# Modulation weights as the moving operand, and the mixer's shift added to z, in a one-core hybrid encoder layer

## The chip, the cores and the metric

The kernel runs on one core of a Trainium2 chip. The time is device microseconds (us) of one execution of the whole program. The times before are 2665.93, 2655.82 and 2659.03 us, median 2659.03.

## What is computed

One encoder layer over two request groups, 2048 and 512 positions of 1024 channels (2560 columns in all), with one modulation vector per group:

```python
mod = (silu(c) @ w_ada + b_ada)
shift1, scale1, gate1, shift2, scale2, gate2 = split(mod, 6)
h = rmsnorm(x, g_mix_norm) * (1 + scale1) + shift1
z = h @ w_in
y_f = fourier_mixer(z[..., :512], w_fourier, b_fourier)
y_s = s5_mixer(z[..., 512:], a, log_dt, b, c, d, w_glu, b_glu)
merged = concat([rmsnorm(y_f), rmsnorm(y_s)])
x = x + gate1 * (merged @ w_out)
h = rmsnorm(x, g_mlp_norm) * (1 + scale2) + shift2
ff = square(relu(h @ w_mlp_in + b_mlp_in)) @ w_mlp_out + b_mlp_out
x = x + gate2 * ff
y = rmsnorm(x, g_final)
```

`w_ada` is 1024 x 6144, `w_in` and `w_out` are 1024 x 1024, the MLP's matrices 1024 x 4096 and back. Results are float32; most products are formed from a high and a low half of each operand (three TensorE matmuls each, lines 229 to 231, from a CAST on ScalarE, L225, and a difference on VectorE, L226).

## The kernel before

Channels lie on partitions, positions along the free axis. The instructions of all stages are written in Python and then ordered, engine by engine, by a list scheduler with a time model of its own, so that an edit in one place can move instructions in another. The stages, with where they lie in the profiled execution:

- **The mixer's start** (`mix_in`, 0 to about 342 us). `ada1` computes the first 16 columns of 128 of the modulation (shift1 in `mod[:, 0:8]`, scale1 in `mod[:, 8:16]`) in four groups `j` of 512 outputs: the two columns of `cs` (silu of c) are the stationary operand, the weights move (L705), the [2, 512] result is copied out (L707) and turned by four transposes (`pat`, L710), VectorE adds the bias (L711). After the fourth group come `gs1` (L712) and `sh4`. `ssm_params` and `ssm_pre` make the tables of the S5 mixer (`Ir`, `Ii`, `O`, `cbi`, `Dm` and others; lines 159 to 319). `zs(it, t)` makes z for one of five tiles of 512 positions, order 4, 0, 1, 2, 3: per k of 8 a scale by `gs1` and the row factor `rb` (L829), then h = x + shift as high half on ScalarE (L831) and low half on VectorE (L832), then 4 x 8 x 3 matmuls into `ps`, a copy to `z` and a store. `folds` prepares the Fourier half with `wfold`'s folded weights `wf`. Loads of the first tile and of `w_in` wait on GpSimd `gate` copies that read a column of `mod` of group `j`, so that they start behind the modulation's weights; `JD = 2` is the group for those that name none.
- **The S5 stage** (about 342 to 660 us). `run` goes over blocks `q` of the S5 mixer (`lead`, `step1` to `step3`: psV, psY) and calls `slot` between them, which runs one `ada_slot` and one unit of `beside` (`fourier`: px, pyc, pys, pc; then `out_f`: pof, which lasts to 762 us). `ada(j)`, j = 16 to 47, makes one more column of 128 of the modulation: eight products of 128 x 128 weights (stationary) with the two columns of `cs` (L687; each product shows as two matmuls in the trace), bias by VectorE (L688). Its weights `wa` are 512 KB a load, `AB = 2` buffers, and `ada_slot` loads the weights of j + 2 after it has used those of j.
- **The mixer's end** (`mix_out`, about 762 to 1020 us): GELU, GLU (`pgate`), the output projection (`pf`/`pout` at L1220 and L1224). `precombine` (L1258 loads, L1263 GpSimd sums, L1264 stores) makes 32 pieces of the MLP's combined weights here, in tiles `q`, while others still wait.
- **The MLP** (`mlp`, from about 1020 us): seven-product (Strassen) blocks; per step a weight load `wr` (L1394), its halves `wh` (ScalarE, L1404) and `wl` (VectorE, L1406), matmuls `pf` and `acc`. In the first block the low halves are also stored (`wL`, L1408). `x` is first scaled and shifted (L1324, L1325), then split into `th` (L1356, L1357). The remaining 12 pieces of `precombine` run in the first block, in slices of a tile `big` (`pre2`); where their loads stand in the queue of SP is left to the scheduler.

Of the kernel before, what the change touches and what calls it, by code (L numbers as in the profile page):

```python
# [26 lines left out]
AB = 2  # L27
# [3 lines left out]
XB = 2  # L31
WB = 4
U0 = 6
JD = 2
XK = 2
CB = 2
NB = 4
# [522 lines left out]
class Net:  # L560
# [3 lines left out]
    def run(self):  # L564
        tc, nc, A = self.tc, self.nc, self.A
        with ExitStack() as es:
# [23 lines left out]
            spps, spp = pool("spp", "right")  # L590
            fes, fe = pool("fe", "right")
            self.Ze = [fe.tile([96, n], F32R, name="Ze%d" % n) for n in (352, 256)]
            self.aj, self.wa = 16, {}
            self.pcs = [(w, c) for w in range(2) for c in range(16)]
            P = self.mix_in(spp)
            sas, sa = pool("ssa", "right")
# [6 lines left out]
            for q in range(nb + 2):  # L603
                if q < nb:
                    bl.append(S.lead(q))
                    self.slot(gen)
                if 1 <= q <= nb:
                    S.step2(bl[q - 1])
                if q >= 2:
                    self.slot(gen)  # L610
                    S.step3(bl[q - 2])
                    self.slot(gen)
                if q < nb:
                    S.step1(bl[q])
                    self.slot(gen)
            self.pull(gen, 1000)
            self.banks(7)
            sps.close()
# [61 lines left out]

    def ada(self, j):
        nc = self.nc
        v3 = lambda n: self.v[n].unsqueeze(2).broadcast_to([128, 8, 2])
        ps = self.ps([128, 2], "pa")
        w = self.wa.pop(j)
        for k in range(8):
            nc.tensor.matmul(ps, w[:, k], self.cs[:, k], start=k == 0, stop=k == 7)  # L687
        nc.vector.tensor_scalar(self.mod[:, j], ps, self.v["b_ada"][:, j:j + 1], None, op0=ALU.add)  # L688
        if j == 39:
            nc.vector.scalar_tensor_tensor(self.gs2, self.mod[:, 32:40], 1.0, v3("g_mlp_norm"), op0=ALU.add, op1=ALU.mult)  # L690
        if j == 47:
            nc.vector.tensor_scalar(self.ng2, self.mod[:, 40:48], -1.0, None, op0=ALU.mult)
            nc.vector.tensor_tensor(self.gb2, self.mod[:, 40:48], v3("b_mlp_out"), op=ALU.mult)

    def ada1(self, tp):

        nc = self.nc
        v3 = lambda n: self.v[n].unsqueeze(2).broadcast_to([128, 8, 2])
        for j in range(4):
            ps = self.ps([2, 512], "pa")  # L700
            for k in range(4):
                w = tp.tile([128, 2, 512], F32, tag="wa", name="wa", bufs=WB)
                nc.sync.dma_start(w, self.A["w_ada1"][j, k])
                for i in range(2):
                    nc.tensor.matmul(ps, self.cs[:, 2 * k + i], w[:, i], start=k + i == 0, stop=k + i == 4)  # L705
            r = tp.tile([2, 512], F32, tag="ar", name="ar")
            nc.scalar.copy(r, ps)  # L707
            pt = self.ps([128, 4, 2], "pat")
            for i in range(4):
                nc.tensor.transpose(pt[:, i], r[:, 128 * i:128 * i + 128], self.ident[:2, :2])  # L710
            nc.vector.tensor_tensor(self.mod[:, 4 * j:4 * j + 4], pt, self.v["b_ada"][:, 4 * j:4 * j + 4].unsqueeze(2).broadcast_to([128, 4, 2]), op=ALU.add)  # L711
        nc.vector.scalar_tensor_tensor(self.gs1, self.mod[:, 8:16], 1.0, v3("g_mix_norm"), op0=ALU.add, op1=ALU.mult)  # L712
        nc.vector.tensor_scalar(self.sh4, self.mod[:, 0:8], 4.0, None, op0=ALU.mult)

    def ada_slot(self):
        j = self.aj
        if j < self.aend:
            self.ada(j)
            if j + AB < self.aend:
                self.ada_load(self.adp, j + AB, AB)  # L720
            self.aj += 1

    def ada_open(self, tp, end):
# [34 lines left out]
    def mix_in(self, spp):  # L758
# [5 lines left out]
        with ExitStack() as es:  # L764
# [9 lines left out]
            def load(t):  # L774
                xs[t] = xp.tile([128, 8, 4, 130], F32, tag="xq", name="xq")
                if t != order[0]:
                    self.gate(xs[t][:1, 0, 0, 0:1], t == order[1])
                    nc.sync.dma_start(xs[t][:, :, :, 0:128], A["xq"][t].rearrange("p k (s n) -> p k s n", s=4))
                    return
                for k in range(0, 8, XK):  # L780
                    self.gate(xs[t][:1, k, 0, 0:1], j=0)
                    nc.gpsimd.dma_start(xs[t][:, k:k + XK, :, 0:128], A["xq"][t][:, k:k + XK].rearrange("p k (s n) -> p k s n", s=4))

            def norm(t):
# [20 lines left out]
            pre = pres.enter_context(tc.tile_pool(name="pre", bufs=1, side="right"))  # L805
            with tc.tile_pool(name="mir", bufs=1) as rp:
                with tc.tile_pool(name="tp0", bufs=1, side="right") as tp0:
                    self.ada1(rp)
                    P = ssm_params(nc, tc, spp, po, pre, tp0, A)
                    load(4)  # L810
                    norm(4)
                    ws = [wp.tile([128, 8, 512], F32R, name="wi%d" % i) for i in range(2)]
                    for k in range(0, 8, 2):
                        raw = rp.tile([128, 2, 512], F32, name="raw", bufs=2)
                        self.gate(raw[:1, 0, 0:1], k < 4, 0)
                        nc.gpsimd.dma_start(raw, A["w_in"][1, :, k:k + 2])
                        split(nc, ws[0][:, k:k + 2], ws[1][:, k:k + 2], raw)
            def zs(it, t):
                b = t // 4
                x = xs[t]  # L820
# [6 lines left out]
                h4 = [i.rearrange("p k (s n) -> p k s n", s=4) for i in h]  # L827
                for k in range(8):
                    v.scalar_tensor_tensor(x4[:, k], x4[:, k], self.gs1[:, k, b:b + 1], rb, op0=ALU.mult, op1=ALU.mult)  # L829
                    sh = self.mod[:, k, b:b + 1]  # L830
                    nc.scalar.activation(h4[0][:, k], x4[:, k], AF.Identity, bias=sh)  # L831
                    v.scalar_tensor_tensor(h4[1][:, k], x4[:, k], sh, h4[0][:, k].bitcast(F32), op0=ALU.add, op1=ALU.subtract)  # L832
                if t % 4 == 0:
                    nc.gpsimd.tensor_copy(x[:, :, 1, 128:129], x[:, :, 2, 0:1])
                    nc.gpsimd.memset(x[:, :, 3, 128:129], 0.0)
# [2 lines left out]
                for m in range(4):  # L838
# [2 lines left out]
                    for k in range(8):  # L841
                        mm3(nc, ps, [i[:, k, ms] for i in ws], [i[:, k] for i in h], k == 0, k == 7)
                    z = hp.tile([128, 8, 64], F32, tag="z", name="z", bufs=2)
                    nc.scalar.copy(z.rearrange("p t (j c) -> p t j c", j=8), ps.rearrange("p (c j t) -> p t j c", j=8, t=8))
                    nc.sync.dma_start(self.uD[128 * m:128 * m + 128, :, 64 * t:64 * t + 64], z)

            def folds(t):
# [418 lines left out]
    def mlp(self):  # L1266
# [12 lines left out]
        with tc.tile_pool(name="mp1", bufs=1, side="right") as t1, tc.tile_pool(name="mp", bufs=1, side="right") as tp:  # L1279
# [110 lines left out]
            def raw(i):  # L1390
                st = steps[i]
                w = A["w%d" % st["ph"]] if st["kind"] == "raw" else self.wS[st["ph"] - 1]
                raws[i] = mw.tile([128, 2, 512], F32, tag="wr", name="wr", bufs=3)
                nc.sync.dma_start(raws[i].rearrange("p a b -> p (a b)"), w[st["j"], st["m"] // 2])  # L1394
                los[i] = mw.tile([128, 2, 512], F32R, tag="wl", name="wl", bufs=3)
                if st["bl"] is not blocks[0]:
                    nc.sync.dma_start(los[i].bitcast(F32), trail(st))
# [109 lines left out]
            def pre2(c):  # L1507
                if c == 0:
                    bl = blocks[0]
                    bl["sc"] = big(bl, "21").rearrange("p a b -> p (a b)")  # L1510
                t = blocks[0]["sc"]
                self.precombine(lambda n, i: t[:, 512 * (i + 4 * (c % 3)):512 * (i + 4 * (c % 3)) + 512])
            for c in range(len(self.pcs)):
                at(P0 + (60 - P0) * c // len(self.pcs), pre2, c)
            for st in steps:
# [33 lines left out]
```

## Time and profile before

| stage, us of the span | PE busy | DVE busy | ACT busy | POOL busy | granted clock | DMA share |
|---|---|---|---|---|---|---|
| 0 to 342 | 285.45 | 274.71 | 144.25 | 74.09 | 0.89 | 0.57 |
| 342 to 660 | 310.34 | 253.64 | 180.99 | 10.49 | 0.84 | 0.58 |
| 660 to 762 | 89.83 | 41.73 | 42.71 | 38.46 | 0.93 | 0.71 |
| 762 to 1020 | 245.26 | 197.41 | 109.41 | 112.22 | 0.97 | 0.82 |

The profiled execution took 2665.03 us, its span is 2663.3 us, and the mean granted clock 0.954. PE is TensorE, DVE VectorE, ACT ScalarE, POOL GpSimd, SP the queue that issues most loads. The granted clock is TensorE's, as a share of 2.4 GHz; at half of that it runs at 1.2 GHz, and a mean between 0.5 and 1 says which part of a stretch lay at either level. Busy time adds up a stage's instructions, so a share below the stage's length is where an engine waited.

### The profile page before, as it was taken

The numbers are of one execution on the slowest core, as the hardware profiler recorded it, in microseconds if no ns is written. First come the engines' busy times: TensorE is split into PE (matmuls) and PEld (weight loads), VectorE is DVE, ScalarE is ACT, GpSimd is POOL, SyncE is SP. The second block draws the span as 40 slices with busy tenths as digits, with TensorE's granted clock in tenths as the row PEclk, the third lists the DMA queues.
The fourth block names the chain that finished last, engine by engine and source line by source line (L and its number), as shares of the span: only waits on it lengthen the run. The fifth ranks groups of instructions, "written<-read, shape, count | busy, mean of one in ns | idle before, by whom it ended". The sixth has DMA issues, their size and how long they took to land.

```text
span 2663.3 us, 35333 instructions
## 1 busy us (share of the span) xinstructions
PE 2530.6 (95%) x12643; PEld 2285.1 (86%) x12643; DVE 1683.9 (63%) x2775; ACT 1293.1 (49%) x2267; POOL 478.7 (18%) x406
## 2 busy tenths in 40 slices
PE   6889999999989999799999999999999999999997
PEld 2778878778767779689999999999999999999997
DVE  7888778776638866758867973354456433634454
ACT  2643466564534425525544557355445573654443
POOL 4410010000346430940400002004000020130000
PEclk8789988879999999899999999999999999999998
DMA  8644476455678978997666777676667766766664
GB/s 293 205 146 113 141 246 214 163 171 184 206 274 268 308 253 288 339 365 277 233 218 216 276 257 251 228 273 230 226 230 276 248 243 226 274 226 227 226 222 163
DMA packets 279040, 627.31 MB, mean 236 GB/s; under 512 B 66512, under 2 KB 110608, under 8 KB 277072
## 3 DMA queue, kind: packets, MB, share of 16 engines
q1 hardware_dynamic: 238416, 549.13, 60.3%
q10 hardware_dynamic: 34096, 61.32, 6.2%
q0 software_dynamic: 6352, 14.60, 1.7%
q8 instruction: 100, 1.64, 0.3%
q14 instruction: 76, 0.62, 0.1%
HBM read 469.10 MB, written 155.85 MB: 235 GB/s over the span
## 4 chain that ended last, share of the span: by engine, by line
PE 68%; DVE 12%; DMA 10%; ACT 4%; issue 4%; POOL 2%; ACTq 0%; SPq 0%; DVEq 0%; POOLq 0%
PE acc L231 9%; PE acc L230 9%; PE acc L229 9%; PE pf L231 8%; PE pf L230 8%; PE pf L229 8%; PE pa L687 2%; PE psY L382 2%; PE psV L350 1%; DMA xq<-in_xq 1%; POOL q L1263 1%; DMA wS<-q 1%; DMA q<-in_w 1%; DVE wl L1406 1%; PE pof L229 1%
## 5 line engine op out<-in xcount | busy, mean ns | idle before, releaser
L1404 ACT CAST wh<-wr 128x512 fp32r<-128x512 f32 x672 | 413.4, 620 | 689.3 <-PE acc L230 342.7
L229 PE MATMUL pf<-th,wh 128*128 128x426 f32 (+1 forms) x1344 | 483.2, 360 | 19.7 <-ACT wh L1404 19.6
L230 PE MATMUL pf<-th,wh 128*128 128x426 f32 (+1 forms) x1344 | 482.2, 359 | 1.0 <-DVE th L1357 1.0
L231 PE MATMUL pf<-th,wl 128*128 128x426 f32 (+1 forms) x1344 | 477.3, 359 | 5.2 <-DVE wl L1406 5.1
L230 PE MATMUL acc<-th,wh 128*128 128x426 f32 (+1 forms) x1344 | 478.4, 357 | 0.3 <-DVE th L1357 0.3
L229 PE MATMUL acc<-th,wh 128*128 128x426 f32 (+1 forms) x1344 | 474.5, 357 | 0.0
L231 PE MATMUL acc<-th,wl 128*128 128x426 f32 (+1 forms) x1344 | 466.9, 357 | 2.1 <-DVE wl L1406 2.0
L1424 DVE TENSOR_TENSOR big<-big,pf 128x426 f32<-128x426 f32 (+1 forms) x320 | 185.1, 596 | 237.2 <-PE pf L231 191.6
L1357 DVE TENSOR_TENSOR th<-big,th 128x1704 fp32r<-128x1704 f32 (+1 forms) x82 | 158.8, 1936 | 201.8 <-ACT th L1356 201.5
L229 PEld LDWEIGHTS pf<-th,wh 128*128 128x128 f32 x1344 | 254.3, 189 | 32.8 <-ACT wh L1404 23.4
L231 PEld LDWEIGHTS pf<-th,wl 128*128 128x128 f32 x1344 | 254.3, 189 | 18.0 <-DVE wl L1406 9.1
L230 PEld LDWEIGHTS pf<-th,wh 128*128 128x128 f32 x1344 | 254.7, 190 | 10.1 <-DVE th L1357 1.4
L231 PEld LDWEIGHTS acc<-th,wl 128*128 128x128 f32 x1344 | 253.2, 189 | 11.2 <-DVE wl L1406 2.8
L230 PEld LDWEIGHTS acc<-th,wh 128*128 128x128 f32 x1344 | 252.5, 188 | 9.5 <-DVE th L1357 1.1
L229 PEld LDWEIGHTS acc<-th,wh 128*128 128x128 f32 x1344 | 252.9, 188 | 9.0
L750 POOL TENSOR_TENSOR r<-r,mh 128x4 f32<-128x4 f32 (+3 forms) x32 | 35.3, 1109 | 1145.1 <-DVE r L749 1145.1
L1431 POOL TENSOR_TENSOR big<-big 128x426 f32<-128x426 f32 (+1 forms) x128 | 142.6, 1118 | 493.4 <-ACT big L1430 490.1
L1406 DVE TENSOR_TENSOR wl<-wr,wh 128x512 fp32r<-128x512 f32 x224 | 174.9, 799 | 62.6 <-ACT wh L1404 62.1
L1263 POOL TENSOR_TENSOR q<-q,q 128x512 f32<-128x512 f32 x80 | 138.4, 1730 | 79.6 <-DMA q<-in_w 57.4
L1356 ACT CAST th<-big 128x1704 fp32r<-128x1704 f32 (+1 forms) x82 | 132.5, 1616 | 0.7 <-PE acc L231 0.7
L1357 DVE TENSOR_TENSOR th<-x,th 128x1704 fp32r<-128x1704 f32 (+1 forms) x23 | 47.5, 2066 | 69.3 <-ACT th L1356 69.3
L1430 ACT ACTIVATE big<-big 128x426 f32<-128x426 f32 (+1 forms) x128 | 71.3, 559 | 38.7 <-DVE big L1424 35.5
(444 smaller groups left out, 4453.4 us busy)
## 6 DMA issues: line engine op xcount, KB each, us to landing
wl<-wL SPq DMA_DIRECT2D x224, 512.0 KB, 3.5
wr<-wS SPq DMA_DIRECT2D x192, 512.0 KB, 4.5
wr<-in_w SPq DMA_DIRECT2D x144, 512.0 KB, 4.4
wL<-wl SPq DMA_DIRECT2D x112, 512.0 KB, 3.4
wa<-in_w_ada SPq DMA_DIRECT2D x48, 512.0 KB, 4.7
q<-in_w SPq DMA_DIRECT2D x80, 256.0 KB, 4.3
wS<-q ACTq DMA_DIRECT2D x80, 256.0 KB, 3.7
big<-x1D SPq DMA_DIRECT2D x8, 1704.0 KB, 7.8
```

Of the source, the lines that this page charges most:

```text
L229: nc.tensor.matmul(out, l[0], r[0], start=start, stop=False)
L230: nc.tensor.matmul(out, l[0], r[1], start=False, stop=False)
L231: nc.tensor.matmul(out, l[1], r[0], start=False, stop=stop)
L382: nc.tensor.matmul(py, m, x[:, j], start=i == 0, stop=i == 2)
L1263: e.tensor_tensor(o, x, y, op=op)
L1356: nc.scalar.copy(th[0], src)
L1357: return th, v.tensor_tensor(th[1], src, th[0].bitcast(F32), op=ALU.subtract)
L1404: nc.scalar.copy(hi, r)
L1406: v.tensor_tensor(lo, r, hi.bitcast(F32), op=ALU.subtract)
L1424: v.tensor_tensor(f[q], f[q], ps, op=op)
L1430: nc.scalar.activation(f[q], f[q], AF.Relu)
L1431: nc.gpsimd.tensor_tensor(f[q], f[q], f[q], op=ALU.mult)
```

## The change

Three edits. (1) In `ada` the operands swap: the two columns of `cs` are stationary and 128 columns of the weights move, so that the result is [2, 128]; ScalarE copies it into the first two rows of the used weight tile, one transpose (`pat`) turns it, and VectorE adds the bias one slot later (`ada_turn`). Since the weight tile is now held for longer, `ada_slot` loads the weights of j + 1, not j + 2, and does so after it has turned those of j - 1. (2) `ada1` makes scale1 first (groups 2, 3), then shift1 (0, 1); gates wait for the group that is now the first. Tokens are only scaled, and their halves are a plain split; shift1 times `w_in` is made once by 24 matmuls (`zshift`), turned, and added as a bias where z is copied out. (3) `pre2` tells the scheduler to put the loads of `precombine` behind the latest weight load.

```diff
-JD = 2
+JD = 1
...
     def ada(self, j):
-        ps = self.ps([128, 2], "pa")
+        ps = self.ps([2, 128], "pa")
         w = self.wa.pop(j)
         for k in range(8):
-            nc.tensor.matmul(ps, w[:, k], self.cs[:, k], start=k == 0, stop=k == 7)
+            nc.tensor.matmul(ps, self.cs[:, k], w[:, k], start=k == 0, stop=k == 7)
+        r = w[:2, 0]
+        nc.scalar.copy(r, ps)
+        self.ada_turn()
+        self.turn = (j, r)
+
+    def ada_turn(self):
...
+        (j, r), self.turn = self.turn, None
+        ps = self.ps([128, 2], "pat")
+        nc.tensor.transpose(ps, r, self.ident[:2, :2])
         nc.vector.tensor_scalar(self.mod[:, j], ps, self.v["b_ada"][:, j:j + 1], None, op0=ALU.add)
...
-    def ada1(self, tp):
+    def ada1(self, tp, js):
-        for j in range(4):
+        for j in js:
...
-        nc.vector.scalar_tensor_tensor(self.gs1, self.mod[:, 8:16], 1.0, v3("g_mix_norm"), op0=ALU.add, op1=ALU.mult)
-        nc.vector.tensor_scalar(self.sh4, self.mod[:, 0:8], 4.0, None, op0=ALU.mult)
+        if js[0]:
+            nc.vector.scalar_tensor_tensor(self.gs1, self.mod[:, 8:16], 1.0, v3("g_mix_norm"), op0=ALU.add, op1=ALU.mult)
+        else:
+            nc.vector.tensor_scalar(self.sh4, self.mod[:, 0:8], 4.0, None, op0=ALU.mult)
+
+    def zshift(self, tp, ws):
+        sh = [self.cp.tile([128, 8, 2], F32R, name="sh%d" % i) for i in range(2)]
+        split(nc, sh[0], sh[1], self.mod[:, 0:8])
+        ps = self.ps([2, 512], "pa")
+        for k in range(8):
+            mm3(nc, ps, [x[:, k] for x in sh], [x[:, k] for x in ws], k == 0, k == 7)
+        r = tp.tile([2, 512], F32, tag="ar", name="ar")
+        nc.scalar.copy(r, ps)
+        pt = self.ps([128, 4, 2], "pat")
+        for i in range(4):
+            nc.tensor.transpose(pt[:, i], r[:, 128 * i:128 * i + 128], self.ident[:2, :2])
+        self.zsh = self.cp.tile([128, 4, 2], F32, name="zsh")
+        nc.vector.tensor_copy(self.zsh, pt)
...
             self.ada(j)
-            if j + AB < self.aend:
-                self.ada_load(self.adp, j + AB, AB)
+            if 16 < j <= self.aend - AB:
+                self.ada_load(self.adp, j + AB - 1, AB)
...
-                    self.gate(xs[t][:1, k, 0, 0:1], j=0)
+                    self.gate(xs[t][:1, k, 0, 0:1], j=2)
...
-                    self.ada1(rp)
-                    P = ssm_params(nc, tc, spp, po, pre, tp0, A)
+                    self.ada1(rp, (2, 3))
                     load(4)
                     norm(4)
...
-                        self.gate(raw[:1, 0, 0:1], k < 4, 0)
+                        self.gate(raw[:1, 0, 0:1], k < 4, 2)
...
+                    self.ada1(rp, (0, 1))
+                    self.zshift(rp, ws)
+                    P = ssm_params(nc, tc, spp, po, pre, tp0, A)
...
-                    sh = self.mod[:, k, b:b + 1]
-                    nc.scalar.activation(h4[0][:, k], x4[:, k], AF.Identity, bias=sh)
-                    v.scalar_tensor_tensor(h4[1][:, k], x4[:, k], sh, h4[0][:, k].bitcast(F32), op0=ALU.add, op1=ALU.subtract)
+                    split(nc, h4[0][:, k], h4[1][:, k], x4[:, k])
...
-                    nc.scalar.copy(z.rearrange("p t (j c) -> p t j c", j=8), ps.rearrange("p (c j t) -> p t j c", j=8, t=8))
+                    nc.scalar.activation(z.rearrange("p t (j c) -> p t j c", j=8), ps.rearrange("p (c j t) -> p t j c", j=8, t=8), AF.Identity, bias=self.zsh[:, m, b:b + 1])
...
-                nc.sync.dma_start(raws[i].rearrange("p a b -> p (a b)"), w[st["j"], st["m"] // 2])
+                self.wload = nc.sync.dma_start(raws[i].rearrange("p a b -> p (a b)"), w[st["j"], st["m"] // 2])
...
-                self.precombine(lambda n, i: t[:, 512 * (i + 4 * (c % 3)):512 * (i + 4 * (c % 3)) + 512])
+                with tc.issue_after(self.wload.ins):
+                    self.precombine(lambda n, i: t[:, 512 * (i + 4 * (c % 3)):512 * (i + 4 * (c % 3)) + 512])
```

The order of the instructions moves at many places; three of them matter below. The first is VectorE (DVE) in the mixer's start, around the first tile. `L829` (`L864` after the change) scales the tokens `xq`, `h` is the low half, `mod<-pat` ends a group of the modulation. Before:

```order
L318 TENSOR_TENSOR O<-O,o_834 128x512
L268 TENSOR_TENSOR Ii<-Ii,cbi 128x512
L711 TENSOR_TENSOR mod<-pat,vec 128x8
L317 TENSOR_TENSOR o_838<-Cr,PWoi 128x512
L267 TENSOR_TENSOR cbi<-Bbi,PWir 128x512
L712 SCALAR_TENSOR_TENSOR gs_97<-mod,vec 128x16
L318 TENSOR_TENSOR O<-O,o_838 128x512
L268 TENSOR_TENSOR Ii<-Ii,cbi 128x512
L829 SCALAR_TENSOR_TENSOR xq<-xq,gs_97,rb 128x4x128 x8
```

And with the change:

```order
L226 TENSOR_TENSOR h_661<-xq,h_660 128x512 x8
L267 TENSOR_TENSOR cbi<-Bbi,PWir 128x512
L730 TENSOR_SCALAR sh_101<-mod 128x16
L226 TENSOR_TENSOR sh_304<-mod,sh_303 128x16
L318 TENSOR_TENSOR O<-O,o_876 128x512
L268 TENSOR_TENSOR Ii<-Ii,cbi 128x512
L317 TENSOR_TENSOR o_931<-nCi,PWoi 128x512
L267 TENSOR_TENSOR cbi<-Bbi,PWir 128x512
L929 COPY wf<-rawf 128x2
L932 TENSOR_TENSOR wf<-rawf 128x255
L931 TENSOR_TENSOR wf<-rawf 128x255
L746 COPY zsh<-pat 128x8
```

The scaling and the split of the first tile now stand ahead of the shift's modulation, and the copy `zsh<-pat`, which needs the 24 matmuls of `zshift`, stands seven rows of tables behind the split of the shift.

The second is TensorE (PE) in the S5 stage, around two `ada` slots. Before:

```order
L350 MATMUL psV<-un,It 128x320 x2
L687 MATMUL pa<-cs,wa 128x2 x16
L382 MATMUL psY<-un,Th 128x320
L382 MATMUL psY<-S,O 128x320 x2
...
L382 MATMUL psY<-S,O 128x320 x2
L687 MATMUL pa<-cs,wa 128x2 x16
L350 MATMUL psV<-un,It 128x320 x3
```

And with the change:

```order
L350 MATMUL psV<-un,It 128x320 x2
L687 MATMUL pa<-wa,cs 2x128 x8
L702 MATMUL pat<-ident,wa 128x2
L687 MATMUL pa<-wa,cs 2x128 x8
L702 MATMUL pat<-ident,wa 128x2
L382 MATMUL psY<-un,Th 128x320
L382 MATMUL psY<-S,O 128x320 x2
...
L382 MATMUL psY<-S,O 128x320 x2
L687 MATMUL pa<-wa,cs 2x128 x8
L702 MATMUL pat<-ident,wa 128x2
```

Two runs of eight products stood back to back before and do now; between them there is now a transpose, behind which the load of the next weights stands.

The third is the MLP's start, on DVE and on SP. DVE before (`x_...` is the MLP's input, `xo` the residual):

```order
L1324 SCALAR_TENSOR_TENSOR x_6810<-x_6810,gs_98,rb 128x428 x14
L1229 TENSOR_TENSOR ss<-ss,sq 128x512
L1224 SCALAR_TENSOR_TENSOR xo<-pout,mod,xo 128x512
L1220 SCALAR_TENSOR_TENSOR xo<-pf,mod,xo 128x512
L1324 SCALAR_TENSOR_TENSOR x_6810<-x_6810,gs_98,rb 128x428 x2
L1406 TENSOR_TENSOR wl<-wr,wh 128x512 x4
L1220 SCALAR_TENSOR_TENSOR xo<-pf,mod,xo 128x512
L1224 SCALAR_TENSOR_TENSOR xo<-pout,mod,xo 128x512
L1357 TENSOR_TENSOR th_9179<-x_6810,th_9178 128x1712
```

DVE with the change; the first row is the last one that reads the output projection's `pout`:

```order
L1257 SCALAR_TENSOR_TENSOR xo<-pout,mod,xo 128x512
L1357 SCALAR_TENSOR_TENSOR x_6944<-x_6944,gs_98,rb 128x428 x15
L1262 TENSOR_TENSOR ss<-ss,sq 128x512
L1357 SCALAR_TENSOR_TENSOR x_6944<-x_6944,gs_98,rb 128x428
L1439 TENSOR_TENSOR wl<-wr,wh 128x512 x4
L782 TENSOR_SCALAR r<-pn 128x4
L1390 TENSOR_TENSOR th_9313<-x_6944,th_9312 128x1712
```

SP a little later, before:

```order
L1394 DMA wr<-in_w 128x1024
L1408 DMA wL<-wl 128x1024
L1394 DMA wr<-in_w 128x1024
L1258 DMA big_9177<-in_w 128x512 x12
L1408 DMA wL<-wl 128x1024 x2
L1394 DMA wr<-in_w 128x1024 x2
```

And with the change:

```order
L1427 DMA wr<-in_w 128x1024
L1291 DMA big_9311<-in_w 128x512 x4
L1441 DMA wL<-wl 128x1024
L1427 DMA wr<-in_w 128x1024
L1291 DMA big_9311<-in_w 128x512 x2
L1441 DMA wL<-wl 128x1024
L1291 DMA big_9311<-in_w 128x512 x2
L1427 DMA wr<-in_w 128x1024
```

The scaling of the MLP's input has moved from ahead of the last outputs of the projection to behind all of them, and the run of twelve loads is broken into runs of two and four.

## Rows read from the trace of the kernel before

**Rows 1.** The page's head, and its TensorE clock in 40 slices.

```profile
span 2663.3 us, 35333 instructions
...
PEclk8789988879999999899999999999999999999998
```

**Rows 2.** Windows by stage: start:end, length, busy time of each engine (instructions), PEclk, DMA share, GB/s.

```profile
342.00:660.00 318.00, 310.34 (x1521) 253.80 (x1520) 253.64 (x684) 180.99 (x438) 10.49 (x15) 0.84 0.58 192
...
1020.00:1190.00 170.00, 144.90 (x702) 132.46 (x702) 108.82 (x122) 76.44 (x134) 96.24 (x66) 0.94 0.95 345
1190.00:2663.00 1473.00, 1454.76 (x7492) 1403.67 (x7490) 807.55 (x1050) 739.31 (x1136) 147.18 (x140) 0.99 0.68 239
```

**Rows 3.** Windows of the mixer's start, same columns.

```profile
10.00:30.00 20.00, 15.18 (x39) 3.18 (x38) 14.65 (x122) 3.25 (x6) 5.81 (x13) 0.95 0.91 303
...
60.00:80.00 20.00, 14.29 (x50) 11.65 (x51) 20.00 (x27) 15.04 (x36) 10.87 (x8) 0.52 0.52 170
80.00:100.00 20.00, 16.21 (x81) 13.61 (x79) 15.21 (x39) 9.40 (x28) 3.11 (x3) 0.74 0.59 191
```

**Rows 4.** Groups by line, DVE, 20 to 345 us: busy, mean ns | idle before.

```profile
L829 DVE SCALAR_TENSOR_TENSOR xq<-xq,gs,rb 128x512 f32<-128x512 f32 x40 | 32.5, 879 | 8.0 <-DMA xq<-in_xq 8.0
L832 DVE SCALAR_TENSOR_TENSOR h<-xq,mod,h 128x512 fp32r<-128x512 f32 x40 | 29.7, 787 | 0.0
```

**Rows 5.** Tile `pa`: durations min/median/max in ns, first and last start.

```profile
L687 PE MATMUL pa<-cs,wa x512: 165/251/354, 345.3 to 656.3; 128*128 128x2 f32 x171
...
L705 PE MATMUL pa<-wa,cs x64: 591/592/1061, 5.8 to 48.6; 128*2 128x512 f32 x64
```

**Rows 6.** The chain of waits, 340 to 430 us: start, length, what.

```profile
372.31 2.40 PE pa L687 x22
...
387.19 0.89 PE pc L999 x8
...
407.58 2.63 PE pa L687 x24
413.80 0.43 PE pyc L229
```

**Rows 7.** Windows of the S5 stage.

```profile
376.00:386.00 10.00, 10.00 (x35) 7.79 (x35) 9.64 (x31) 4.99 (x17) 1.59 (x3) 0.51 1.07 322
386.00:410.00 24.00, 24.00 (x149) 20.57 (x147) 22.76 (x61) 18.45 (x42) 1.50 (x2) 0.99 0.71 227
410.00:417.00 7.00, 7.00 (x21) 5.46 (x22) 6.52 (x22) 4.08 (x18) 1.08 (x2) 0.52 1.17 379
...
505.00:513.00 8.00, 5.32 (x13) 3.27 (x14) 6.09 (x9) 7.31 (x18) 0.00 (x0) 0.79 0.75 304
513.00:525.00 12.00, 12.00 (x54) 9.88 (x53) 10.45 (x28) 5.23 (x15) 0.00 (x0) 0.72 0.58 186
```

**Rows 8.** The page's DMA issues: KB each, median us from issue to landing.

```profile
wa<-in_w_ada SPq DMA_DIRECT2D x48, 512.0 KB, 4.7
```

**Rows 9.** The chain of waits, 1010 to 1140 us.

```profile
1009.96 2.38 DVE x L1324 x4
1012.34 0.60 DVE ss L1229
...
1015.41 2.41 DVE wl L1406 x4
...
1019.15 1.86 DVE th L1357
1021.05 0.46 PE pf L230
```

**Rows 10.** The timeline around 1057 us, queue of SP: start, issuing time, line, loads.

```profile
1056.99 6.70 SPq L1258 DMA_DIRECT2D big<-in_w  x12
```

**Rows 11.** Windows of the MLP's first block.

```profile
1076.00:1087.00 11.00, 5.23 (x16) 4.58 (x17) 8.14 (x5) 5.45 (x11) 11.00 (x8) 0.54 0.89 336
```

**Rows 12.** Waits of PE, 1015 to 1190 us: us in total, times, longest.

```profile
PE pf L229 <- ACT wh L1404: 19.6, 5, 9.9
```

More of the change, by code (lines that the diff above doesn't have):

```diff
@@ L592, in run @@
             self.Ze = [fe.tile([96, n], F32R, name="Ze%d" % n) for n in (352, 256)]
-            self.aj, self.wa = 16, {}
+            self.aj, self.wa, self.turn = 16, {}, None
             self.pcs = [(w, c) for w in range(2) for c in range(16)]
@@ L682, in ada @@
         nc = self.nc
-        v3 = lambda n: self.v[n].unsqueeze(2).broadcast_to([128, 8, 2])
-        ps = self.ps([128, 2], "pa")
+        ps = self.ps([2, 128], "pa")
         w = self.wa.pop(j)
         for k in range(8):
-            nc.tensor.matmul(ps, w[:, k], self.cs[:, k], start=k == 0, stop=k == 7)
+            nc.tensor.matmul(ps, self.cs[:, k], w[:, k], start=k == 0, stop=k == 7)
+        r = w[:2, 0]
+        nc.scalar.copy(r, ps)
+        self.ada_turn()
+        self.turn = (j, r)
+    def ada_turn(self):
+        nc = self.nc
+        if not self.turn:
+            return
+        (j, r), self.turn = self.turn, None
+        v3 = lambda n: self.v[n].unsqueeze(2).broadcast_to([128, 8, 2])
+        ps = self.ps([128, 2], "pat")
+        nc.tensor.transpose(ps, r, self.ident[:2, :2])
         nc.vector.tensor_scalar(self.mod[:, j], ps, self.v["b_ada"][:, j:j + 1], None, op0=ALU.add)
@@ L711, in ada1 @@
             nc.vector.tensor_tensor(self.mod[:, 4 * j:4 * j + 4], pt, self.v["b_ada"][:, 4 * j:4 * j + 4].unsqueeze(2).broadcast_to([128, 4, 2]), op=ALU.add)
-        nc.vector.scalar_tensor_tensor(self.gs1, self.mod[:, 8:16], 1.0, v3("g_mix_norm"), op0=ALU.add, op1=ALU.mult)
-        nc.vector.tensor_scalar(self.sh4, self.mod[:, 0:8], 4.0, None, op0=ALU.mult)
+        if js[0]:
[3 more added lines that the diff above has]
+    def zshift(self, tp, ws):
+        nc = self.nc
+        sh = [self.cp.tile([128, 8, 2], F32R, name="sh%d" % i) for i in range(2)]
[10 more added lines that the diff above has]
+        nc.vector.tensor_copy(self.zsh, pt)
     def ada_slot(self):
```

## Prediction

> **What bounds the kernel now.** I read the page's head first, then busy time by stage, then in each stage the chain of waits and the granted clock. The stages have different limits. From 1190 us to the end PE is busy 1454.76 of 1473 us [rows 2]; nothing in the change touches that stretch, so its 1473 us stand. 7492 matmuls in 1473 us make 0.197 us each, the pace that the MLP's first block would have if nothing stopped it. It doesn't: between 1020 and 1190 us PE shows 702 matmuls, worth 138 us at that pace, in 170 us. About 32 us are lost there; PE waits 19.6 us for `wh`, in five waits with one of 9.9 us [rows 12], and after the long one the clock is 0.54 for 11 us [rows 11].
>
> The S5 stage is PE's too, 310.34 of 318 us [rows 2], but its clock is only 0.84. The clock has two levels, so a mean of 0.84 says that 0.32 of 318 us, 102 us, ran at 1.2 GHz. Work at that level takes twice its time, so 51 us are lost there. DVE, at 253.64 us, comes next. In the mixer's start it is DVE that is full: 20.00 of 20 us from 60 to 80 us, with PE at a clock of 0.52 [rows 3]. The page's clock line shows the two dips, its second slice and slices six to nine [rows 1].
>
> **Part 1: `ada`, the S5 stage.** First the clock. PE isn't idle before it falls: in 386 to 410 us it is busy 24.00 of 24 us at 0.99, and from 410 us it runs at 0.52 [rows 7]. What it did just before was a run of 24 old `ada` matmuls from 407.58 us [rows 6]. Likewise 22 of them from 372.31 us, and 0.51 from 376 us. I counted fifteen such falls up to 762 us, and eleven follow runs of 12 to 32 of these matmuls within 7 us. The same products in the other form, weights moving, stand in `ada1` [rows 5]: while they run, between 10 and 30 us, the clock is 0.95 though PE is busy only 15.18 of 20 us [rows 3]. I take it that the two-column moving operand lowers the clock. The new form moves 128 columns. So 11/15 of 51 us, 37 us, can come back.
>
> The matmuls themselves cost the same: 24 old ones take 2.63 us, 0.110 each, and 8 with 128 moving columns take 0.89 us, 0.111 each [rows 6]. Added are 32 transposes, at most two such slots of 0.111 us each, say 3 us with waits; 32 copies on ScalarE (busy 180.99 of 318 us) hide beside other work.
>
> The Trainium skill speaks against this gain: "TensorE: Matmul & The Clock Gate", part 1 on the clock gate, says that the chip sets the clock by how busy TensorE has been lately, and that idle periods lower it. By that rule an engine busy 24.00 of 24 us would not fall, and swapping operands would give 0 instead of 37 us; the rows above disagree, unless the chip counts a two-column matmul as little activity. It stays as a rival.
>
> Then the loads. A weight load takes 4.7 us from issue to landing (median) [rows 8], and now only one is under way: the load for j + 1 waits until the transpose of j - 1 has read its buffer. With 0.6 us for issue and semaphores PE needs 5.3 us of other work between two `ada`s. I walked PE's new order with the pitches of the trace (0.43 us for 512 columns at half, half of that at full clock [rows 6]). Seven of 30 places have less; two have nothing (the order above shows two `ada`s with just a transpose between). The shortfalls (1.6, 0.7, 1.1, 2.7, 5.3, 4.4, 5.3) sum to 21 us. Before, two loads were ahead and PE lost 7.7 us in the whole stage [rows 2]. So S5: -37 + 21 + 3 = **-13 us**. The bounds: -34 if all loads hide, +24 if no fall goes away.
>
> **Part 2: shift behind the tokens.** Saved on DVE: 40 L832, 787 ns each [rows 4], become plain differences of 512 columns, 0.60 us [rows 9]: 7 us by means, at most; DVE is full only in part of it, and is waiting for loads 8.0 us at L829 alone. Gained early: the first tile no longer waits for four groups of the modulation. Against it: PE now meets the 24 `zshift` matmuls before the tables' transposes; at half clock, 0.43 us each, 10 us, at full 5. DVE must wait for `zsh<-pat` in its order, with seven rows of table work to cover (about 5 us at 0.60 to 0.9 us a row). Uncovered are 4 to 9 us, and what queues behind is DVE's table work, on which `ssm_pre`'s stores and PE's later rows wait. From 80 to 100 us DVE is busy 15.21 of 20 us [rows 3], so half of a delay is caught up. I take **+2 us**, between -6 (all of DVE's saving counts) and +10 (the stall counts whole).
>
> **Part 3: the MLP's start.** Before, 14 of 16 scalings of the MLP's input stood ahead of the last `pout` rows on DVE, and PE went from `pout` to `pf` at 1021.05 us without a stop. Now all 16 stand behind the last `pout`. PE then has nothing until DVE is through 16 scalings (four take 2.38 us [rows 9], so 9.5), `ss` 0.60, four `wl` 2.41 and `th` 1.86: 14.4 us, with semaphores and the row factor's small steps 16. After it some 2 us go at 1.2 GHz, as after the 9.9 us wait. **+18 us**, as far as DVE's order binds; +10 if ScalarE and PE work that I count as following is really moved into the gap.
>
> **Part 4: the loads of `precombine`.** Before, SP issued 12 of them in one go for 6.70 us [rows 10], and the weight loads behind them came late. Now runs are of two to four, with weight loads between. The 32 us lost can't all come back: 1020 to 1190 us moves 345 GB/s at a DMA share of 0.95 [rows 2], 58.7 MB, and the highest rate of a stretch in these rows is 379 GB/s [rows 7], by which the same bytes take 155 us. **-15 us**, between 0 and -32.
>
> The profiled execution took 2665 us (its span 2663.3 [rows 1]), 6 us over the median of three, 2659. Sum: 2 - 13 + 18 - 15 = -8 us, 2657 for an execution like the profiled one, and **2651 us** against the median.
>
> **Rivals.** *A, the forecast*: gains and losses nearly cancel, 2651, own range 2637 to 2665. Chance 0.43.
>
> *B, the clock comes back and the loads hide.* S5 gives -34, since PE runs late anyway and slots have work of `beside` in front, and the burst gives 23 instead of 15: 2 - 34 + 18 - 23 = -37, 2622. For it: eleven of fifteen falls follow the old form, and most places in the order have over 6 us of other work. Against it: DVE's 253.64 us leave at most 64 us between it and the stage, and faster PE makes every load later. Chance 0.22.
>
> *C, slower: late weights bring the clock down again.* Before, a wait did this: from 505 to 513 us PE is busy 5.32 of 8 us, and the clock is then 0.72 for 12 us [rows 7]. If each short place is followed by a stretch like 376 to 386 us (10 us, 5 lost), n of them add 5n to -8. From n = 2 the sum is above zero, from n = 5 it is over 13 us slower; at 6 or 7 it is +22 to +27, 2681 to 2686, and 2680 with some of it hidden. For it: two of the places have no cover at all. Against: most shortfalls are under 3 us. The Trainium skill's same page, in its part on clock oscillation, describes short groups of matmuls between waits for loads that bring the clock down each time; the trace agrees with the row of 505 us, by which it costs 5 us a time. Chance 0.20.
>
> *D, little happens.* The clock does not follow the form of the operand (the rule of the page above), and loads hide by the same slowness: S5 costs 3 us, not -13, and the sum is +8, 2667. The same comes out if runs of four loads hold up the weights as twelve did (2 - 13 + 18 = +7). So the change would not do what it says. Chance 0.15.
>
> **How the numbers follow.** About 0.5%, 13 us, can be told from no change: faster means below 2646, slower above 2672. Faster: a third of A (0.15), all of B (0.22), little else: 0.37. Slower: C (0.20) and a fifth of D (0.03): 0.23. Same: 0.40. The range goes from a little under B to C: 2618 to 2682; it leaves out B's far end (S5 and the start at both their bounds) and C with more falls.
>
> **What would show it.** In the S5 stage the clock rises from 0.84 to above 0.92, and no fall follows an `ada` run; PE waits for `wa` appear, of some 15 to 21 us. In the start, DVE waits at `zsh<-pat` and h's low half takes 0.6 us. At the MLP's start PE stands idle for about 16 us behind the last `pout`. In the first block the runs of 12 loads are gone, and PE's waits for `wh` shrink from 19.6 us to under 10. Wrong would be: a clock still at 0.84 (step 1), no idle PE before `pf` (step 3), or waits for `wh` as long as before (step 4).

## The result and the profile after

The changed kernel takes 2684.86 us (median; 2681.9 to 2691.0) beside 2661.17 us for the kernel before on the same chip: ratio 1.0093, 95% interval 1.0065 to 1.012. It is slower by about 24 us, where 2651 with a range of 2618 to 2682 was forecast. The profiled execution's span is 2689.2 us, 25.9 more than before, at a higher mean clock (0.966 after 0.954). The page's head and clock line of the changed kernel:

```profile
span 2689.2 us, 35514 instructions
...
PEclk8789999989999997999999999999999999999998
```

Of the dip of the slices six to nine [rows 1] only slice nine is left, a new one stands at slice sixteen (the MLP's start), and the kernel is slower. Where the time went shows in the first and last starts of TensorE's tiles (`ps`: z; `psV` to `psY`: the S5 stage; `pgate`, `pout`: the mixer's end; `pf`: the MLP):

| us of the span | before | after | change of the stretch |
|---|---|---|---|
| first matmul of z | 64.9 | 95.7 | |
| first psV (start ends) | 331.9 | 352.0 | +20.1 |
| last psY (S5 blocks end) | 654.4 | 707.0 | |
| first pgate | 761.9 | 775.2 | -6.8 |
| last pout | 1019.4 | 1033.7 | +1.0 |
| first pf | 1019.7 | 1056.3 | +22.3 |
| last pf | 2380.1 | 2406.8 | -9.9 |

The stretches sum to +26.7 us; the rest up to the end takes 0.8 less. Windows of the changed kernel (columns as in rows 2):

```profile
60.00:80.00 20.00, 7.89 (x24) 2.16 (x24) 14.09 (x27) 3.91 (x7) 11.50 (x8) 0.62 0.29 92
80.00:100.00 20.00, 9.84 (x42) 8.97 (x43) 8.45 (x16) 7.52 (x23) 3.81 (x3) 0.57 0.79 250
352.00:707.00 355.00, 321.70 (x1686) 238.38 (x1686) 260.76 (x694) 201.40 (x501) 16.26 (x24) 0.96 0.57 182
1034.00:1056.00 22.00, 1.99 (x9) 1.78 (x8) 19.88 (x32) 13.50 (x24) 0.00 (x0) 0.59 0.75 254
1056.00:1190.00 134.00, 121.94 (x570) 111.54 (x571) 80.36 (x85) 66.04 (x118) 79.14 (x54) 0.93 0.91 324
1190.00:2663.00 1473.00, 1465.96 (x7545) 1412.66 (x7544) 812.52 (x1043) 742.16 (x1140) 161.95 (x150) 1.00 0.69 244
```

From 60 to 100 us, where DVE was busy 35.2 of 40 us before and PE 30.5 [rows 3], DVE is now busy 22.5 and PE 17.7. In the S5 blocks the clock is 0.96 instead of 0.84 [rows 2]. From 1034 to 1056 us PE does nearly nothing.

**The start.** What PE waited for, 0 to 362 us (who waited for what, us in total, times, longest):

```profile
PE pa L229 <- ACT sh L225: 13.6, 1, 13.6
PE pat L744 <- ACT ar L741: 11.2, 1, 11.2
...
PE pa L231 <- DVE sh L226: 4.9, 1, 4.9
```

All three are steps of `zshift`. The 11.2 us lead to another place: its copy `ar` (L741) could run at 78.6 us, when the 24 matmuls were done, and ran at 89.20. The timeline of ScalarE (idle time before in brackets), and the same of VectorE and of SP's queue:

```profile
87.89 0.63 ACT L833 ACTIVATE xn<-xn 128x512 f32<-128x512 f32 x1 [22.16 <-DMA xn<-in_xn]
...
89.20 0.56 ACT L741 COPY ar<-pa 2x512 f32<-2x512 f32 x1
```

```profile
89.23 0.17 DVE L929 COPY wf<-rawf 128x2 f32<-128x2 f32 x1 [15.15 <-DMA rawf<-in_w_in]
...
90.43 0.17 DVE L746 COPY zsh<-pat 128x8 f32<-128x8 f32 x1 [0.37 <-PE pat L744]
```

```profile
74.15 0.65 SPq L811 DMA_DIRECT2D xq<-in_xq  x1
74.84 9.09 SPq L832 DMA_DIRECT2D xn<-in_xn  x2
84.03 0.85 SPq L927 DMA_DIRECT2D rawf<-in_w_in  x2
```

ScalarE stood 22 us at the second tile's rows `xn`, in front of `ar`, and VectorE 15 us at the folded weights `rawf`, in front of `zsh`. Both loads wait for a gate on GpSimd. Its timeline before and after (line 636, now 637, is `gate`):

```profile
44.44 0.31 POOL L636 COPY xq<-mod 1x1 f32<-1x1 f32 x1
44.69 0.45 POOL L636 COPY xn<-mod 1x1 f32<-1x1 f32 x2
45.09 1.26 POOL L636 COPY rawf<-mod 1x1 f32<-1x1 f32 x2
```

```profile
65.57 6.01 POOL L637 CAST shf<-mod 1x1 fp32r<-1x1 f32 x1
71.52 2.60 POOL L637 COPY xq<-mod 1x1 f32<-1x1 f32 x1
74.07 0.29 POOL L637 COPY xn<-mod 1x1 f32<-1x1 f32 x2
...
74.92 0.29 POOL L637 COPY rawf<-mod 1x1 f32<-1x1 f32 x2
```

`JD = 1` names the group of the modulation that is now done fourth, at 65.35 us on VectorE; `JD = 2` named the one done third. The loads start some 30 us later: 24 us lie between the ends of the two groups, and GpSimd's queue adds the rest, since its copies for `shf` and `xq` (6.01 and 2.60 us) stand in front of those for `xn`.

**The MLP's start.** PE's waits from 1020 to 1200 us:

```profile
PE pn L769 <- DVE ss L1262: 19.7, 1, 19.7
PE pf L229 <- ACT wh L1437: 6.2, 6, 3.2
```

The wait is the one that was forecast, and `ss` stands behind 15 scalings on DVE. Why these come so late shows in what bounds the MLP's memory. The pool of GELU's tiles, in which `precombine`'s tiles `q` lie too, opens on memory that the S5 stage gives back; the MLP's pool opens when that pool closes. Last `psY`, loads of `q`, first load of the MLP's weights, before and after:

```profile
L382 PE MATMUL psY<-S,O x128: 430/432/741, 395.7 to 654.4; 128*128 128x320 f32 x128
...
L1258 SPq DMA_DIRECT2D q<-in_w x80: 327/370/999, 680.3 to 972.8; - x80
...
L1394 SPq DMA_DIRECT2D wr<-in_w x144: 328/333/1448, 1000.5 to 2619.2; - x144
```

```profile
L382 PE MATMUL psY<-S,O x128: 430/432/537, 421.5 to 707.0; 128*128 128x320 f32 x128
...
L1291 SPq DMA_DIRECT2D q<-in_w x80: 327/333/3301, 734.6 to 1024.4; - x80
...
L1427 SPq DMA_DIRECT2D wr<-in_w x144: 328/337/1325, 1040.1 to 2645.9; - x144
```

The twenty pieces take 292.5 us before and 289.8 after (283 to 293 in every kernel of this document that has twenty of them here); they start 26 and 28 us behind the last `psY` (23 to 30 in every kernel). With the S5 blocks ending 52.6 us later, the MLP's first weights are loaded 39.6 us later, behind the last `pout`.

What released the first load into the MLP's pool, that of the row factor `rb` which the scalings read, stands among SP's waits, before (975 to 1022 us) and after (1020 to 1060 us):

```profile
SPq L1318 <- DVE mg L226: 1.3, 1, 1.3
```

```profile
SPq L1351 <- DMA wS<-q: 0.5, 1, 0.5
```

Before, the last store `wS` of a piece had landed at 982.1 us, and this load came at 999.6, behind the last reader (VectorE's `mg`) of another tile of the closing pool. After, the store lands at 1039.1 us and the load comes at 1039.2: now the pieces are what the MLP waits for.

### The profile page after: what moved, and what is told of

The parts are those of the page before. It is cut to its first block, busy times and chain, and to the rows that moved or that the text cites. A ratio compares the mean times of both kernels' runs of the same rounds, so it can differ in the third digit from the quotient of the medians.

```text
span 2689.2 us, 35514 instructions
## 1 busy us (share of the span) xinstructions
PE 2511.0 (93%) x12703; PEld 2241.0 (83%) x12703; DVE 1685.3 (63%) x2777; ACT 1298.0 (48%) x2301; POOL 476.7 (18%) x406
## 4 chain that ended last, share of the span: by engine, by line
PE 65%; DMA 12%; DVE 11%; ACT 4%; issue 4%; POOL 2%; SPq 1%; ACTq 0%; DVEq 0%; POOLq 0%
PE acc L231 9%; PE acc L230 9%; PE acc L229 9%; PE pf L231 8%; PE pf L230 8%; PE pf L229 8%; PE pa L687 2%; PE psY L382 1%; DMA wa<-in_w_ada 1%; DMA xq<-in_xq 1%; PE pof L231 1%; PE pof L230 1%; PE pof L229 1%; DVE wl L1439 1%; DMA pf<-pD 1%
## 5 line engine op out<-in xcount | busy, mean ns | idle before, releaser
L231 PEld LDWEIGHTS pf<-th,wl 128*128 128x128 f32 x1344 | 254.6, 189 | 21.6 <-DVE wl L1439 12.7
L231 PEld LDWEIGHTS acc<-th,wl 128*128 128x128 f32 x1344 | 253.2, 189 | 11.2 <-DVE wl L1439 2.8
L783 POOL TENSOR_TENSOR r<-r,mh 128x4 f32<-128x4 f32 (+3 forms) x32 | 36.3, 1140 | 1154.2 <-DVE r L782 1064.8
L1296 POOL TENSOR_TENSOR q<-q,q 128x512 f32<-128x512 f32 x80 | 128.7, 1609 | 94.6 <-DMA q<-in_w 79.7
```

The lines of the kernel that those rows point to most:

```text
L231: nc.tensor.matmul(out, l[1], r[0], start=False, stop=stop)
L1296: e.tensor_tensor(o, x, y, op=op)
```

## The experiments

Each of the kernels below was compared with the kernel before on the same chip (medians 2660 to 2662 us). The stretches given for a run are those of its one profiled execution. In five of them two loads of `wa` are ahead again; this edit, called **two ahead** below, is

```diff
-        r = w[:2, 0]
-        nc.scalar.copy(r, ps)
         self.ada_turn()
+        r = self.ones[:2, 8:136]
+        nc.scalar.copy(r, ps)
...
-            if 16 < j <= self.aend - AB:
-                self.ada_load(self.adp, j + AB - 1, AB)
+            if j + AB < self.aend:
+                self.ada_load(self.adp, j + AB, AB)
```

with the tile `ones` 136 columns wide.

**1. The changed kernel, gates on the group done third** (`JD = 1` to `JD = 0`).

> The changed kernel with JD = 0: the gates that named the last group of the modulation (j = 1, done fourth) name the one that is done third (j = 0), as in the kernel before. Theory 'late gates' (the loads of the second tile and of the folded weights start 29 us later, and ScalarE and VectorE wait for them ahead of the shift's copies): the first matmul of z moves from 95.9 us to about 75 to 80, the S5 stage starts at about 337 us instead of 352, and the whole comes to about 2668 to 2672. Rival 'shift's own chain' (24 matmuls, copy and transposes in front of the tables' transposes cost it): the first matmul of z stays above 90 us and the time at 2682 to 2687.

Measured: 2689.79 us, ratio 1.0111 (1.0089 to 1.0134). The wait at `wf` is gone and the start is back: the first matmul of z at 82.1 us, psV at 336.2, 15.8 us earlier than in the changed kernel. So the gates were what the start lost most by. But nothing of it arrived: the way to `pgate` is 6.4 us longer, to the last `pout` 4.9, the gap at the MLP 7.3. The S5 blocks end at 708.5 us, no earlier than with the late start. The theory holds for its place and fails for the time.

**2. The kernel before, gates on the fourth group** (`JD = 2` to `JD = 3`).

> The kernel before with one number changed, JD = 3: its gates wait for the fourth group of the modulation instead of the third. Late gates: the second tile's load starts at about 57 us instead of 44.8, and the S5 stage 5 to 12 us later, 2666 to 2673. Rival: loads that come 12 us later are still early enough, 2659 to 2664, and then late gates cost only beside the shift's chain.

Measured: 2662.00 us, ratio 1.0013 (0.9996 to 1.003). The S5 stage starts 6.1 us later (338.0), and `pgate` comes 5.4 us earlier (756.5). A late start of this size is taken up in this order (the rival).

**3. The first edit alone.**

> The kernel before with the first edit alone (weights of ada moving, one load ahead). Theory: the S5 stage gives back some 7 us or more, and the idle TensorE before the MLP, some 22 us, comes with this edit too since the planner's order after it has all 16 scalings behind the last output: 2666 to 2676. Rival: the idle time comes from the third edit, and this one alone gives 2648 to 2656.

Measured: 2707.87 us, ratio 1.0181 (1.0158 to 1.0204), slower than both kernels and than both theories said. The start is that of before (psV at 331.9), the S5 blocks end at 707.3, the first load of `q` is at 735.9, and PE waits 20.8 us before the first `pf` at 1060.1. So the gap comes with the first edit, and the first block then loses some 40 us to its burst of loads as well.

**4. The changed kernel, two ahead.**

> The changed kernel with the [2, 128] result of ada copied to spare columns of another tile, so that the weights' buffer is free after its matmuls and two loads are ahead as before. Theory: waits for wa in the S5 stage go (about 15 us), with the clock kept high; the order at the MLP's start is that of the kernel before again, so the idle 22 us go, and the run of 12 loads comes back (10 us lost): 2685 - 15 - 22 + 10, about 2658. Rival: one load ahead cost nothing, and only the order changes: 2670 to 2675.

Measured: 2660.53 us, ratio 0.9995 (0.9979 to 1.0011): the whole loss is gone, by an edit that leaves the start as late as it was (psV at 349.6). Its S5 window, its waits at the MLP's start, and its chain of pieces:

```profile
350.00:665.00 315.00, 300.93 (x1624) 221.08 (x1622) 254.58 (x688) 196.13 (x493) 15.71 (x23) 0.99 0.62 203
```

```profile
PE pf L229 <- ACT wh L1437: 19.2, 4, 9.4
PE pf L231 <- DVE wl L1439: 7.0, 9, 1.5
```

```profile
L1291 SPq DMA_DIRECT2D q<-in_w x80: 327/370/2685, 688.7 to 973.4; - x80
...
L1427 SPq DMA_DIRECT2D wr<-in_w x144: 332/335/1248, 987.4 to 2611.0; - x144
```

The S5 blocks end at 664.7 us, 42.3 earlier than with one load ahead, no wait of PE for `wa` is left in the stage, the first `pf` follows the last `pout` within 0.6 us, and the burst of twelve loads, with its waits for `wh`, is back.

**5. The changed kernel with 16 pieces ahead of the MLP** (`PCG = 20` to `PCG = 16`).

> The changed kernel with PCG = 16: four of the 20 pieces of precombine that run ahead of the MLP are left for its first block. Theory 'chain of pieces': the S5 stage's end (707 us) lets the pool of GELU's tiles and of the pieces open, 20 pieces take some 290 us whatever the kernel, and only then the MLP's pool opens; with 16 pieces the MLP's first matmul comes right behind the last pout, at about 1034 us instead of 1056, without the 19.7 us wait; the first block loses more to its burst of loads (16 to 28 us instead of some 20): 2665 to 2680. Rival 'DVE order of its own': the 16 scalings still stand behind the last pout, first matmul at 1050 or later, 2685 or more.

Measured: 2695.81 us, ratio 1.0144 (1.0117 to 1.0172). The MLP starts right behind the last `pout`, as the theory of the pieces has it: 16 pieces take 239 us instead of 290, and `pf` starts at 1021.5 us, 2.4 us behind it. That is earlier than the theory's 1034, since the last `pout` itself came 14.6 us earlier (the first `pgate` 7.1). The rows of `q` and `wr`:

```profile
L1291 SPq DMA_DIRECT2D q<-in_w x64: 327/333/3266, 727.1 to 966.1; - x64
...
L1427 SPq DMA_DIRECT2D wr<-in_w x144: 328/336/1708, 1001.3 to 2647.5; - x144
```

The price was too low: first to last `pf` takes 1386.9 us, 36.4 more than in the changed kernel. Sixteen more loads of 256 KB with their sums and stores cost the first block more than the gap did.

**6. The first edit, two ahead, alone.**

> The kernel before with the first edit alone, and two loads ahead (the result of ada copied to spare columns of another tile). Theory: clock above 0.95 in the S5 stage with few waits for wa, the S5 stage over 15 to 30 us earlier than in the kernel before (654 us), and the MLP's start bound by pout: 2640 to 2650. Rival: the time from there on is bound by the pieces and by the loads of the first block, and the gain is lost there: 2655 to 2662.

Measured: 2658.31 us, ratio 0.9983 (0.9968 to 0.9998), the rival's side: the clock of the way to `pgate` is 0.96, `pgate` comes 13.2 us earlier (748.7), and the first block gives 7.2 us of it back (first to last `pf` 1367.6).

**7. The changed kernel, two ahead and `JD = 0`.**

> The changed kernel with two loads ahead, and with its gates on the group that is done third (JD = 0). Late gates cost the start 13 to 16 us, and here nothing later is bound by one load ahead: 2660 - 13 = about 2647 (2642 to 2652). Rival: the start's gain is taken up again later, 2657 to 2662.

Measured: 2662.91 us, ratio 1.0014 (0.9999 to 1.0029). The start is 12.7 us shorter than in run 4, the way from psV to `pgate` 20.5 us longer. The time is on the rival's side again, 0.9 us above its range.

**8. The second edit alone.**

> The kernel before with the second edit alone (shift behind the tokens, JD = 1), ada and pre2 as before. Late gates and the chain of the shift: S5 stage starts at about 350 us instead of 332; the whole 2661 + 10 to 18 = 2671 to 2679, less if the S5 stage takes it up. Rival: the second edit costs nothing on the path that ends last, 2658 to 2664.

Measured: 2691.66 us, ratio 1.0122 (1.0101 to 1.0142), more than expected: +14.8 us at the start, +4.4 to `pgate` (the old `ada` form, 122 us at the lower clock from 335 to 762 us, 113 in the kernel before), +9.9 in the MLP. Here a late start is not taken up.

**9. The changed kernel without its third edit.**

> The changed kernel without its third edit (the loads of precombine placed by the planner alone). Its order is that of the changed kernel up to the MLP, and there SP issues ten loads in one go again behind the fifth weight load. Theory (the third edit gives back the burst): the MLP's first matmul at 1056 us as in the changed kernel, waits for wh up from 6.2 to 15 us or more, and the time from the MLP's first to the last pf 1360 to 1366 instead of 1350.5: 2685 + 12 = about 2697. Rival (the 22 us without work let the weights run ahead, and the loads' place matters little): 2683 to 2688.

Measured: 2699.37 us, ratio 1.0141 (1.0124 to 1.0159), 14.5 us more than the changed kernel (measured on another chip); first to last `pf` takes 1363.6 us, 13.1 more. PE's waits from 1020 to 1200 us, and SP's queue:

```profile
PE pn L769 <- DVE ss L1262: 20.8, 1, 20.8
PE pf L229 <- ACT wh L1437: 11.5, 8, 2.2
PE pf L231 <- DVE wl L1439: 8.4, 7, 2.7
```

```profile
1061.04 4.93 SPq L1291 DMA_DIRECT2D big<-in_w  x10
```

In this order the third edit is worth nearly the 15 us that it was priced at; the waits for `wh` rose to 11.5 us, less than the 15 expected.

**10. The third edit alone.**

> The kernel before with the third edit alone. In its order SP issues twelve loads in one go as before, since the planner already had them behind the eighth weight load. Theory (the third edit acts only where the planner would put the loads ahead of the weights, as it does after one load ahead): no change, 2655 to 2665, waits for wh near 19.6 us. Rival (it is worth 10 to 15 us in any order): 2645 to 2650.

Measured: 2664.75 us, ratio 1.001 (0.9994 to 1.0026). SP issues its twelve loads in one go at 1053.77 us as before. The edit binds only where the planner would put loads ahead of the weights.

**11 and 12. Two ahead, and the pieces spread in time**, on the kernel before with the first edit, and on the changed kernel:

```diff
-P0 = 4
+P0 = 12
...
-                at(P0 + (60 - P0) * c // len(self.pcs), pre2, c)
+                at(P0 + (72 - P0) * c // len(self.pcs), pre2, c)
```

> The kernel before with the first edit, two loads ahead, and the twelve late pieces of precombine started at steps 12 to 67 instead of 4 to 55, behind the latest weight load: each piece's four loads then stand by themselves between weight loads. Theory (the burst costs the first block 15 us or more): waits for wh down from 20.9 to under 8 us, 2658 - 12 = about 2646 (2640 to 2650). Rival (the first block is bound by the bytes it moves): 2653 to 2660.

> The changed kernel with two loads ahead and the pieces spread likewise. Burst theory: 2660 - 12 = about 2648 (2642 to 2652). Rival (bytes): 2656 to 2662.

Measured: 2653.85 us, ratio 0.9979 (0.9967 to 0.9991), and 2654.16 us, ratio 0.9975 (0.9963 to 0.9987). Both are faster than the kernel before by some 6 us, and the second beats the changed kernel by about 31 us. The waits in the first of them, 1000 to 1220 us:

```profile
PE pf L231 <- DVE wl L1421: 12.7, 13, 1.8
PE pf L229 <- ACT wh L1419: 11.5, 4, 6.6
```

How far the MLP's matmuls are behind a pace of 0.195 us each, by their starts in the traces, in us:

```
matmul number           120    240    360    600    800   1000
before                  4.0   15.3   24.0   38.6   39.7   39.8
changed                 6.1    7.4   14.1   25.1   29.1   29.1
run 9                   5.8   13.6   28.8   39.4   39.5   40.1
run 4                   2.8   13.2   23.0   36.7   42.6   42.6
run 11                  3.3    4.1   16.2   21.9   29.7   40.6
run 12                  4.4    5.2   15.9   20.6   26.0   35.6
run 5 (16 more loads)   3.1   15.0   23.8   43.7   56.9   64.0
```

Spreading the loads puts most of the loss off, from matmul 600 to 1000, and takes 4 to 7 us of it away (run 11 beside run 6's 44.8 at number 1000, run 12 beside run 4). In time, run 11 lies within its rival's range, and run 12 between its theory's and its rival's. So the loss goes mostly with the work that is left for the block (64.0 with sixteen more loads); bunching counts too, as the changed kernel's 29.1 beside the 40.1 of run 9 shows.

## Why the prediction was wrong

By the table, the terms missed so: the start by 18 us (+20.1 for +2), S5 up to `pgate` by 6 (-6.8 for -13), the gap by 4, the loads by 5, the mixer's end by 1; with 0.8 us less at the end this is the 34 us from -8 to the profiled +25.9. The start missed by most, and yet it did not decide the time: run 1 gives back 15.8 us of it and the time stays, run 4 leaves it late and the whole loss goes.

**The step that failed is the S5 term, "-37 + 21 + 3 = -13".** It counted what PE gains and waits for on the way to the stage's end and let nothing hang on that end. The clock's part came true: what the lower clock cost in the blocks went from 0.15 of 323 us to 0.04 of 355, 34 us less (37 forecast), and waits for `wa` were 13.1 us in six places (21 in seven). That 37 came so near is in part luck, since falls counted up to 762 us were set against a loss up to 660. By the trace's clock records, thirteen stretches at 1.2 GHz begin between 342 and 660 us, ten of them within 7 us of 12 to 32 old `ada` matmuls and with PE idle at most 1.1 us of these 7. The ten last 68 us, which is 34 lost.

The swap itself cost more than 3 us: between starts the transposes take 5.0 us, the products, counted at the higher clock, some 4 more (59.1 us instead of 54.7). To `pgate` the stretch gained 6.8 us. But the planner also put 239 instead of 120 `pof` matmuls in front of the last `psY`, 28 us of work at 0.234 us, and PE stood idle 33 instead of 11 us. So the blocks ended at 707.0 us, and the chain of S5's end, twenty pieces and the MLP's pool, which had 17 us of slack before, set the MLP's start.

Run 4 shows it by the one edit that takes the whole loss away. Its blocks are 39.9 us shorter: the changed kernel's have 19 us more idle time, lose 12 us more to the lower clock, and have 46 more `pof` matmuls in front of the last `psY` (11 us). How much of this the late loads cause, and how much the order that the planner made around them, no run separates. Runs 1 and 3 show the chain by ends at 708.5 and 707.3 us with the early start, run 5 by shortening it. With two loads ahead the stretch from psV to `pgate` is 32.3 us shorter than before in run 4, 15.6 in run 6: the -34 of the bounds and of rival B was within reach.

Rival C had the side and the place (late weights) but not the way, and that the time fell on its 2681 to 2686 is luck. Falls of the clock did stand where PE had waited: seven of the eight from 335 to 762 us begin with 2.2 to 4.5 us of idle PE in the 7 us ahead (the eighth, at 389 us, with none), but only two of them stand at a wait for `wa` (495 and 557 us). The eight stretches make 34 us at the lower level and cost 17 us, where those of before cost 56.

**The start, "+2", was mis-sized**: +20.1 us, outside its bounds of -6 and +10. It priced `zshift` and VectorE's table rows, and not the gates: that "the last group" is a later time than "the third", and that two in-order engines would stand at those loads in front of the shift's copies. VectorE's wait stood at `wf` (15.2 us), not at `zsh<-pat` (0.4 us). The low halves did become cheaper (681 ns instead of 787), by 4 us in all and not by 7. Run 1 brings back 15.8 us of it; run 1 and run 7 also show that in the one-ahead and two-ahead orders this doesn't reach the end, while in run 8, with the old `ada`, it does. What takes it up isn't settled: the stretch from psV to `pgate` loses 12 us more to the lower clock in run 1 than in the changed kernel, and in run 7 15 us more than in run 4, with 9 us more of idle time.

**The gap, "+18", was right in size** (22.3 us) and in its row on DVE; that it has its own cause was not. It is the end of the chain above, not an accident of DVE's order: no kernel with two loads ahead has it. In the four kernels with one load ahead and twenty pieces (the changed one, runs 1, 3 and 9) the first load into the MLP's pool follows the landing of the last store of a piece within 0.4 us; in the other ten it comes 2.6 to 23.9 us behind.

**The loads of `precombine`, "-15", were about right**: 13.1 us in the MLP's stretch by run 9, 9.9 beside the kernel before. But the edit does it only after one load ahead (runs 9 and 10).

**The clock**: the rule of the Trainium skill ("TensorE: Matmul & The Clock Gate", part 1), that the clock follows how busy TensorE has been, would have left the S5 stage's falls in place. The trace disagrees as read by PE's busy time: with the moving weights the clock is 0.99 in run 4, where PE is busy 300.93 of 315 us, and was 0.84 where it was busy 310.34 of 318 [rows 2]. The changed kernel's seven falls behind idle time agree with it.

## What to carry to other kernels

Ask of a stage that gets later not only which engine its work fills, but what memory its end gives back: a pool that opens there can start a chain of loads and sums as long as the next stage. An operand swap that holds a buffer longer takes a load out of flight; copy the small result elsewhere before giving up the depth. And where a gate names "the group", look when that group is done after the order is turned.

## What was not expected of the hardware

In the S5 stage of the kernel before, TensorE's clock fell to 1.2 GHz behind runs of the old `ada` matmuls, two columns moving, while TensorE was hardly idle. With 128 columns moving the stage's mean clock is 0.96 in the changed kernel and 0.99 in run 4, instead of 0.84, at nearly the same time from start to start (medians 0.109 and 0.112 us). The four traces with the old form lose 39 to 53 us of the S5 blocks to the lower clock, the ten with the new form 3 to 29. The swap also turned the stationary operand from 128 columns into two; which of the two operands matters, no run separates.

A 1x1 copy on GpSimd took 6.01 us beside eight low halves on VectorE (66.02 to 70.91 us), 0.56 before; run 8 has it again, 6.00 us. What held it was not tried.
